# A diffusion step on one core: in the last feed-forward, the hi weights meet hi and lo of the operand in one product of 512 columns

## The chip, the cores and the metric

The kernel runs on one core of a Trainium2 chip. The metric is the device time of one execution in microseconds (us). Three executions of the kernel before took 2309.35, 2310.64 and 2311.0 us; the median is 2310.64 us.

## The reference

One inference step of a transformer trunk of two layers on two groups of 128 tokens each: context tokens and latent tokens, with the same weights. D_MODEL is 2048, D_FF is 5632. Every layer is a mixer (attention) followed by a gated feed-forward with a convolution over positions, each with its own shift, scale and gate from the conditioning:

```python
def conv_ffn(h, w_up, w_conv, b_conv, w_down):
    u = h @ w_up
    up = jnp.pad(u, ((0, 0), (1, 1), (0, 0)))
    u = up[:, :-2] * w_conv[0] + up[:, 1:-1] * w_conv[1] + up[:, 2:] * w_conv[2] + b_conv
    gate, val = u[..., :D_FF], u[..., D_FF:]
    return (jax.nn.silu(gate) * val) @ w_down
...
        x = x + gt1 * m
        h = rmsnorm(x, g_norm_ffn[l]) * (1 + sc2) + sh2
        x = x + gt2 * conv_ffn(h, w_ffn_up[l], w_ffn_conv[l], b_ffn_conv[l], w_ffn_down[l])
    return rmsnorm(x, g_final), ab_ctx, c_ctx
```

All inputs and outputs are float32. The change concerns the feed-forward of the second and last layer.

## The kernel before

**Operands in two parts.** The matmuls run on the type F32R, which keeps fewer bits than float32. So each operand is split into a hi part (the value rounded to F32R, an ACT copy, line 245) and a lo part (the remainder, a DVE subtraction, line 246). A product is the sum of three: hi weights on hi operand, hi weights on lo operand, lo weights on hi operand. Activations lie features on partitions, tokens along the free dimension: NT = 256 columns, 128 of each group. For each block k of 128 features, `hx[:, k, :NT]` is hi, `hx[:, k, NT:2 * NT]` is lo, and the two lie side by side in a row of ROW = 512 columns. The inner tiles `g` of the feed-forward have the same layout.

**One product.** `gemm` (from line 345) makes one block of 128 output features: it takes a bank of PSUM, `acc`, of which there are three in rotation, and issues for each of the 16 or 22 blocks of weights three matmuls of 256 columns into the first half of the bank. The second half of the bank stays unused. The matmul is issued at line 107, which is a helper, so all products have that line in the profile; they are told apart by the tile names: `hx` in the up-projection, `g` in the down-projection.

**Weights.** `Weights` loads them by DMA on SP's queue in tiles of 16 blocks (`raw`, three buffers), and splits half a tile (8 blocks, 1024 columns) at a time into `wh` and `wl`, which have four buffers each. A split of new weights waits until TensorE has finished with the oldest of the four.

**The feed-forward.** `ffn` (line 1452) runs `up(q)` and `down(gs, q)` for q = 0 and 1, each with half of the 5632 inner features. `up` makes 22 pairs of products (gate and value) of 16 blocks; `conv` takes each product through an ACT activation out of PSUM (line 1482) and two DVE operations that add the shifted neighbours (lines 1485 and 1488), then comes the gate's Silu (line 1504), a multiplication (line 1505), and a split into a tile `g`. `down` makes 16 products of 22 blocks; `residual` adds each one, times its gate, to `x` with two DVE operations that read PSUM (line 830), one for each group. In q = 1 the squares of `x` are also summed for the final normalisation. The last four products of `down` in q = 1 are "quiet": their weights are split in finer pieces.

**Other products.** The first four products of `up(0)` come from the normalisation before (`ready`, up to 258 columns wide). Five more products of `up(0)` begin with a matmul that is 32, 16, 8, 4 or 2 columns wider (`WIDER`). In the attention of the first layer there are products of 384 columns, on the tile `kv_in`.

**Beside it.** In the feed-forward DVE also sums vectors of the modulation from rows of `w_ada` (line 460, 2.3 us each). In the last layer these are needed by the residuals of `down(0)`.

**Order.** The order of the instructions on each engine is set by the framework's planner from its own estimate of their times; only instructions passed to `keep_order` keep the program's order.

Of the kernel before, what the change touches and what calls it, by code (L numbers as in the profile page):

```python
# [14 lines left out]
ALU = mybir.AluOpType  # L15
# [3 lines left out]
P = 128  # L19
# [3 lines left out]
NT = 2 * T  # L23
ROW = 2 * NT
SHIFT = 320
NL = 2
# [65 lines left out]
def step_kernel(ctx: ExitStack, tc: tile.TileContext, A: dict):  # L92
    nc = tc.nc
    dve, act, pool, sp = nc.vector, nc.scalar, nc.gpsimd, nc.sync
    kept = []

    def keep_order(i):
        if not any(i is j for j in kept):
            kept[:] = [i]
            tc.keep_in_program_order(i)  # L100
# [16 lines left out]
    pe = TensorE()  # L117
# [3 lines left out]
    tmp = ctx.enter_context(tc.tile_pool(name="tmp", bufs=2))  # L121
    small = ctx.enter_context(tc.tile_pool(name="small", bufs=4))
    pacc = ctx.enter_context(tc.tile_pool(name="pacc", bufs=3, space=PSUM))
# [5 lines left out]
    def banks(name):  # L129
        return tc.tile_pool(name=name, bufs=1, space=PSUM)  # L130
# [3 lines left out]
    def nm(s):  # L134
        uid[0] += 1
        return f"{s}_{uid[0]}"

    def T_(pl, shape, tag, dt=F32, bufs=None):
        kw = {} if bufs is None else {"bufs": bufs}
        return pl.tile(shape, dt, tag=tag, name=nm(tag), **kw)  # L140
# [11 lines left out]
    def C(name):  # L152
        a, w = _AT[name]
        return cst[:, a:a + w]
# [89 lines left out]
    def split(out_hi, out_lo, src, pin=lambda i: i):  # L244
        pin(act.copy(out_hi, src))  # L245
        pin(dve.tensor_tensor(out=out_lo, in0=src, in1=out_hi.bitcast(F32), op=ALU.subtract))  # L246
# [98 lines left out]
    def gemm(blocks, xh, xl, n=NT, first=0, between=None, more=None):  # L345

        fixed = lambda i: keep_order(i) if between is not None else i
        ps = T_(pacc, [P, 512], "acc")  # L350
        last = len(blocks) - 1
        for i in range(last + 1):
            k = (i + first) % (last + 1)
            wh, wl = blocks[k]
            x0 = more(k) if more and i == 0 else xh(k)
            fixed(pe.matmul(ps[:, :x0.shape[-1]], wh, x0, start=(i == 0), stop=False))
            if callable(between):
                if i == (last + 1) // 2:
                    between()
            elif between and i in between:  # L360
                between[i]()
            fixed(pe.matmul(ps[:, :n], wh, xl(k), start=False, stop=False))
            fixed(pe.matmul(ps[:, :n], wl, xh(k), start=False, stop=(i == last)))
        return ps[:, :n]

# [78 lines left out]
    def load_row():  # L446
        feat["row"] = T_(feat["home"], [P, 2, D], "condb")
        sp.dma_start(out=feat["row"], in_=A["condb"])
        for r in range(2):
            keep_order(act.activation(feat["row"][:, r], feat["row"][:, r], AF.Silu))  # L450
# [30 lines left out]
    class Deep:  # L481
# [44 lines left out]
        def pump(self):  # L526
            self.due += self.rate
            while self.due >= 1.0:
                self.due -= 1.0
                if self.steps:  # L530
                    self.step()
# [82 lines left out]
    def ensure(l, j, qs=range(4)):  # L614
        for u in [(l, j, q) for q in qs]:
            while u in ROWS and u not in done and ada["i"] <= ROWS.index(u):
                row_step()
            while u in FEATS and u not in done:
                feature_step()
            while u in DEEP[l] and u not in done:  # L620
                deep.step()
            while u not in done:
                later.pop(0)()
# [92 lines left out]
    def operand(pl, tag):  # L716
        return home(pl, tag)[:, :KD * ROW].rearrange("p (k n) -> p k n", k=KD)

    def raw_tile(pl, tag):
        return home(pl, tag)[:, :KD * 2 * UW].rearrange("p (k n) -> p k n", k=KD)  # L720
# [731 lines left out]
    def ffn(hx, W, ready, turn, l, st):  # L1452
        xh, xl = (lambda k: hx[:, k, :NT]), (lambda k: hx[:, k, NT:2 * NT])
        wider = list(WIDER)
        long = len(ready) > 3

        def product():
            if ready:
                return ready.pop(0)
            if in_order:  # L1460
                return gemm(W.chunk(), xh, xl, between=in_order.pop(0))
            if wider:
                n = NT + wider.pop(0)
                return gemm(W.chunk(), xh, xl, more=lambda k: hx[:, k, :n])
            return gemm(W.chunk(), xh, xl)

        WD = Weights(A["w_down"][l], KQ, TB)
        cw = ada["cw"]
        with tc.tile_pool(name=f"ffn{l}", bufs=1) as fp, banks(f"pffn{l}") as pf:
            feat["home"], feat["pool"] = fp, pf  # L1470
            feat["due"] = 0.0
            in_order = [{}, {}] + turn + [{}]
            T_(fp, [P, SHIFT // 4], "pad")

            def conv(m):
                early = bool(ready)
                pin = keep_order if early else lambda i: i
                if len(ready) > 4 - 2 * long:
                    W.ahead(pin)
                ps = product()  # L1480
                y = T_(fp, [P, NT], "cv", bufs=3)
                pin(act.activation(y, ps, AF.Identity, scale=cw[:, 1, m:m + 1], bias=cw[:, 3, m:m + 1]))  # L1482
                y3 = y.rearrange("p (g t) -> p g t", g=2)
                p3 = ps.rearrange("p (g t) -> p g t", g=2)
                pin(dve.scalar_tensor_tensor(out=y3[:, :, 1:], in0=p3[:, :, :T - 1],  # L1485
                                             scalar=cw[:, 0, m:m + 1], in1=y3[:, :, 1:],
                                             op0=ALU.mult, op1=ALU.add))
                pin(dve.scalar_tensor_tensor(out=y3[:, :, :T - 1], in0=p3[:, :, 1:],  # L1488
                                             scalar=cw[:, 2, m:m + 1], in1=y3[:, :, :T - 1],
                                             op0=ALU.mult, op1=ALU.add))  # L1490
                if early and ready and not long:
                    W.ahead(pin)
                return y

            def up(q):
                gs = []
                for i in range(q * KQ, (q + 1) * KQ):
                    rate = 0 if i < LATE else FRATE["up"]
                    fine[0] = False
                    gate = conv(i)  # L1500
                    pump(0, rate)
                    val = conv(NFF + i)
                    pump(0, rate)
                    act.activation(gate, gate, AF.Silu)
                    dve.tensor_tensor(out=val, in0=gate, in1=val, op=ALU.mult)
                    g = T_(fp, [P, ROW], "g", F32R, bufs=KQ)
                    split(g[:, :NT], g[:, NT:2 * NT], val)
                    gs.append(g)
                    if i == LATE - 1:
                        load_row()  # L1510
                return gs

            def down(gs, q):
                u, rows = None, None
                if q == NQ - 1 and l < NL - 1:
                    u = raw_tile(keep, "hx")
                    rows = raw_rows(u, l + 1, 0)
                for c in range(KD):
                    quiet = q == NQ - 1 and c >= KD - QUIET[0]
                    fine[0] = quiet  # L1520
                    if q == 0:
                        ensure(l, 5, [c // 4])
                    ps = gemm(WD.chunk(), lambda k: gs[k][:, :NT], lambda k: gs[k][:, NT:2 * NT])
                    if l == NL - 1 and q == NQ - 1 and c == KD - 1:
                        last_residual(ps, l, 1, c, st)
                    else:
                        residual(ps, l, 1, c, st if q == NQ - 1 else None)
                    if rows:
                        rows(c)
                    if l == NL - 1 and q == NQ - 1 and c in EARLY:  # L1530
                        act.activation(x[:, c], x[:, c], AF.Identity, scale=C("gfin")[:, c:c + 1])
                    pump(0, 0 if quiet else FRATE["down"])
                return u

            for q in range(NQ):
                gs = up(q)
                u = down(gs, q)
            while feat["i"] < FLIMIT[stage[0]]:
                feature_step()
            return u  # L1540


    with banks("pab") as ppool["ada"]:
# [3 lines left out]
        ps = T_(pacc, [P, 512], "acc")  # L1547
# [5 lines left out]
        hx = operand(keep, "hx")  # L1553
        st = stat_init()
        with tc.tile_pool(name="beside", bufs=1) as beside:
            o = mixer_ab(hx, beside)
            with tc.tile_pool(name="raw", bufs=1) as rp:
# [3 lines left out]
                W = Weights(A["w_up"][0], KD, 1)  # L1561
# [5 lines left out]
    with tc.tile_pool(name="cc", bufs=1) as cp, banks("pc") as ppool["ada"]:  # L1567
# [3 lines left out]
        W = Weights(A["w_in_c"], KD, 1)  # L1571
# [5 lines left out]
        W = Weights(A["w_up"][1], KD, 1)  # L1577
# [149 lines left out]
```

## Time and profile before

| what | value |
|---|---|
| median of three executions | 2310.64 us |
| profiled execution, its own time | 2308.48 us |
| its span, first to last instruction | 2306.7 us |
| last feed-forward in the chain of waits | 1579.00 to 2294.34 us |
| transfers, mean over the span | 268 GB/s, queue of the loads 72.3% busy |
| granted clock of TensorE, mean | 0.996 |

In a page of the profile PE is TensorE's matmuls, PEld its weight loads, DVE VectorE, ACT ScalarE, POOL GpSimd, SP SyncE. A group of instructions is given by source line, engine, operation, output and input tile, shape and count; then its busy time, the mean of one in ns, and the idle time of the engine just before it with what ended it. A row of the timeline is start, duration, instruction, and how many were merged into the row. A matmul's duration includes the way through the array; the pace is read from the distance of two starts. A row of the stretches of time gives for each engine the busy time and the number of instructions, then the granted clock, the share of busy transfer engines and GB/s.

### The profile page before, as it was taken

How to read it: one execution, taken by the hardware profiler on the slowest of the kernel's cores; microseconds unless marked ns; L12 is line 12 of the kernel's file. 1: busy time of each engine (PE TensorE's matmuls, PEld its weight loads, DVE VectorE, ACT ScalarE, POOL GpSimd, SP SyncE). 2: the span in 40 equal slices, each digit the busy share in tenths (PEclk: the TensorE clock that was granted, in tenths of full speed). 3: DMA queues.
4: the chain of work that ended last, by engine and by line, in shares of the span. 5: the costliest groups of instructions: out<-in, count | busy, mean ns of one | idle time of the engine just before them, and what ended most of it. 6: DMA issues, size and time to landing. Idle time of an engine off the chain costs nothing.

```text
span 2306.7 us, 47528 instructions
## 1 busy us (share of the span) xinstructions
PE 2278.7 (99%) x19504; PEld 2186.1 (95%) x19504; DVE 1887.0 (82%) x2967; ACT 1202.5 (52%) x1973; POOL 188.5 (8%) x238
## 2 busy tenths in 40 slices
PE   8999999999999999999999999999999999999998
PEld 6788878999999999999999999999999999999998
DVE  4667979889999999999988988898899965666654
ACT  4346555665553355555575455457555434555543
POOL 0011211400000000001130000023000000000011
PEclk9999999999999999999999999999999999999999
DMA  9988888777777777777787888776677755555553
GB/s 379 378 334 304 313 326 332 280 275 264 263 256 288 290 276 258 270 264 256 286 310 283 309 316 312 271 268 227 247 256 260 264 200 190 200 190 194 198 188 127
DMA packets 100122, 617.15 MB, mean 268 GB/s; under 512 B 10752, under 2 KB 18880, under 8 KB 33344
## 3 DMA queue, kind: packets, MB, share of 16 engines
q1 hardware_dynamic: 99904, 614.11, 72.3%
q8 instruction: 153, 2.51, 0.4%
q14 instruction: 65, 0.53, 0.1%
HBM read 609.32 MB, written 4.75 MB: 266 GB/s over the span
## 4 chain that ended last, share of the span: by engine, by line
PE 84%; DMA 0%; DVE 0%; ACT 0%; POOL 0%; issue 0%; DVEq 0%; ACTq 0%
PE acc L107 81%; PE ada L107 1%; PE att L107 1%; PE att L110 0%; DMA araw<-w_ada 0%; DVE x L1589 0%; PE ada L110 0%; PE misc L107 0%; DVE wl L246 0%; ACT wh L245 0%; POOL rr L219 0%; DVE hx L246 0%; ACT hx L245 0%; ACT p L862 0%; PE misc L110 0%
## 5 line engine op out<-in xcount | busy, mean ns | idle before, releaser
L107 PE MATMUL acc<-hx,wh 128*128 128x256 f32 (+1 forms) x7264 | 1256.2, 278 | 3.6 <-ACT wh L245 1.7
L245 ACT CAST wh<-raw 128x1024 fp32r<-128x1024 f32 (+2 forms) x828 | 796.1, 972 | 871.3 <-PE acc L107 744.1
L246 DVE TENSOR_TENSOR wl<-raw,wh 128x1024 fp32r<-128x1024 f32 (+2 forms) x828 | 923.2, 1130 | 252.8 <-ACT wh L245 247.8
L107 PEld LDWEIGHTS acc<-hx,wh 128*128 128x128 f32 x7264 | 1100.4, 188 | 23.6 <-issue 8.3
L107 PE MATMUL acc<-hx,wl 128*128 128x256 f32 (+1 forms) x3632 | 1007.1, 277 | 4.7 <-DVE wl L246 4.7
L107 PEld LDWEIGHTS acc<-hx,wl 128*128 128x128 f32 x3632 | 684.5, 188 | 8.5 <-DVE wl L246 6.0
L107 PE MATMUL acc<-g,wh 128*128 128x256 f32 x2816 | 478.8, 276 | 0.0
L107 PEld LDWEIGHTS acc<-g,wh 128*128 128x128 f32 x2816 | 423.8, 188 | 0.0
L107 PE MATMUL acc<-g,wl 128*128 128x256 f32 x1408 | 388.0, 276 | 0.0
L460 DVE CUSTOM_DVE_ANT_0 junk<-araw,condb 128x2048 f32<-128x2048 f32 x128 | 294.1, 2297 | 0.0
L107 PE MATMUL acc<-hxc,wh 128*128 128x256 f32 (+1 forms) x1568 | 282.9, 282 | 0.0
L107 PEld LDWEIGHTS acc<-g,wl 128*128 128x128 f32 x1408 | 264.2, 188 | 0.0
L107 PEld LDWEIGHTS acc<-hxc,wh 128*128 128x128 f32 x1568 | 241.5, 189 | 4.5 <-issue 4.2
L107 PE MATMUL acc<-hxc,wl 128*128 128x256 f32 (+1 forms) x784 | 218.5, 279 | 0.0
L208 POOL TENSOR_TENSOR sqacc<-sqacc,sq 128x256 f32<-128x256 f32 x62 | 72.8, 1174 | 1493.8 <-ACT sq L204 1493.7
L107 PEld LDWEIGHTS acc<-hxc,wl 128*128 128x128 f32 x784 | 147.5, 188 | 0.4
L1482 ACT ACTIVATE cv<-acc,convw 128x256 f32<-128x256 f32 x169 | 94.4, 559 | 0.0
L512 DVE CUSTOM_DVE_ANT_0 hx<-block,condb 128x1024 fp32r<-128x1024 f32 x65 | 79.2, 1218 | 9.0 <-DMA block<-w_ada 6.4
L1488 DVE SCALAR_TENSOR_TENSOR cv<-acc,convw,cv 128x254 f32<-128x254 f32 x169 | 80.8, 478 | 3.2
L830 DVE SCALAR_TENSOR_TENSOR x<-acc,mod,x 128x128 f32<-128x128 f32 x190 | 57.1, 341 | 30.4 <-PE acc L107 30.4
L1485 DVE SCALAR_TENSOR_TENSOR cv<-acc,convw,cv 128x254 f32<-128x254 f32 x169 | 80.1, 474 | 0.0
L107 PE MATMUL ada<-araw,condw 128*32 128x512 f32 (+1 forms) x608 | 73.8, 578 | 1.3 <-DMA araw<-w_ada 1.3
(262 smaller groups left out, 1542.4 us busy)
## 6 DMA issues: line engine op xcount, KB each, us to landing
raw<-w_up SPq DMA_DIRECT2D x176, 1024.0 KB, 4.8
araw<-w_ada SPq DMA_DIRECT2D x136, 1024.0 KB, 5.9
raw<-w_down SPq DMA_DIRECT2D x88, 1024.0 KB, 4.8
raw<-w_in_c SPq DMA_DIRECT2D x48, 1024.0 KB, 6.7
block<-w_ada SPq DMA_DIRECT2D x41, 512.0 KB, 6.4
raw<-w_in_ab SPq DMA_DIRECT2D x18, 1024.0 KB, 9.2
raw<-w_out_ab SPq DMA_DIRECT2D x16, 1024.0 KB, 7.1
raw<-w_out_c SPq DMA_DIRECT2D x16, 1024.0 KB, 6.4
```

Of the source, the lines that this page charges most:

```text
L107: return self.placed(nc.tensor.matmul(*a, **kw))
L208: eng.tensor_tensor(out=st["acc"], in0=st["acc"], in1=sq, op=ALU.add)
L245: pin(act.copy(out_hi, src))
L246: pin(dve.tensor_tensor(out=out_lo, in0=src, in1=out_hi.bitcast(F32), op=ALU.subtract))
L460: keep_order(dve.tensor_tensor_reduce(out=T_(feat["pool"], [P, D], "junk"), in1=feat["row"][:, c], in0=feat["raw"].rearrange("p g n -> p ( ...
L512: keep_order(dve.tensor_tensor_reduce(out=self.junk, in0=self.raw, in1=self.row[:, c].rearrange("p (g n) -> p g n", g=2), scale=1.0, scala ...
L830: dve.scalar_tensor_tensor(out=x[:, c, s], in0=ps[:, s], scalar=mod[:, l, 3 * which + 2, c, g:g + 1], in1=x[:, c, s], op0=ALU.mult, op1=AL ...
L1482: pin(act.activation(y, ps, AF.Identity, scale=cw[:, 1, m:m + 1], bias=cw[:, 3, m:m + 1]))
L1485: pin(dve.scalar_tensor_tensor(out=y3[:, :, 1:], in0=p3[:, :, :T - 1], scalar=cw[:, 0, m:m + 1], in1=y3[:, :, 1:], op0=ALU.mult, op1=ALU.add))
L1488: pin(dve.scalar_tensor_tensor(out=y3[:, :, :T - 1], in0=p3[:, :, 1:], scalar=cw[:, 2, m:m + 1], in1=y3[:, :, :T - 1], op0=ALU.mult, op1=A ...
```

## The change

The new function `gemm_pairs` issues two matmuls for each block of weights in place of three. The hi weights meet all 512 columns of the operand's row, hi and lo, and fill both halves of the bank; the lo weights meet hi and add to the first half. For the last block the order of the two is turned round. Then ACT copies the second half to a tile of SBUF (`nt`, four buffers, which exists before) and DVE adds the first half to it. The caller gets this tile where it got PSUM before.

It is used in the last layer alone, from its first `down` on: 16 products of `down(0)`, 44 of `up(1)` and 12 of `down(1)`. The four quiet products at the end remain as they are.

```diff
+    def gemm_pairs(blocks, both):
+
+        ps = T_(pacc, [P, 512], "acc")
+        last = len(blocks) - 1
+        for k in range(last + 1):
+            wh, wl = blocks[k]
+            two = [(ps, wh, both(k)), (ps[:, :NT], wl, both(k)[:, :NT])]
+            for i, (out, w, xs) in enumerate(two if k < last else two[::-1]):
+                pe.matmul(out, w, xs, start=(k == 0 and i == 0), stop=(k == last and i == 1))
+        t = T_(tmp, [P, NT], "nt", bufs=4)
+        act.copy(t, ps[:, NT:])
+        dve.tensor_tensor(out=t, in0=ps[:, :NT], in1=t, op=ALU.add)
+        return t
...
+        pairs = [False]
 
         def product():
             if ready:
...
+            if pairs[0]:
+                return gemm_pairs(W.chunk(), lambda k: hx[:, k, :ROW])
             return gemm(W.chunk(), xh, xl)
...
-                    ps = gemm(WD.chunk(), lambda k: gs[k][:, :NT], lambda k: gs[k][:, NT:2 * NT])
+                    if pairs[0] and not quiet:
+                        ps = gemm_pairs(WD.chunk(), lambda k: gs[k][:, :ROW])
+                    else:
+                        ps = gemm(WD.chunk(), lambda k: gs[k][:, :NT], lambda k: gs[k][:, NT:2 * NT])
...
             for q in range(NQ):
                 gs = up(q)
+                pairs[0] = l == NL - 1
                 u = down(gs, q)
```

## The prediction

> **What bounds the kernel now.** I read the page first: shares of the engines, then the chain of work that ended last.
>
> ```profile
> PE 2278.7 (99%) x19504; PEld 2186.1 (95%) x19504; DVE 1887.0 (82%) x2967; ACT 1202.5 (52%) x1973; POOL 188.5 (8%) x238
> ...
> PE acc L107 81%; PE ada L107 1%; PE att L107 1%; PE att L110 0%; DMA araw<-w_ada 0%; DVE x L1589 0%; PE ada L110 0%; PE misc L107 0%; DVE wl L246 0%; ACT wh L245 0%; POOL rr L219 0%; DVE hx L246 0%; ACT hx L245 0%; ACT p L862 0%; PE misc L110 0%
> ```
>
> TensorE is busy 99% of the span, and one line of matmuls is 81% of the chain. Next, the chain in order of time over the last stage:
>
> ```profile
> 1579.00 715.33 PE acc L107 x6296
> ```
>
> From 1579.00 us to 2294.34 us, which is the whole last feed-forward, the chain is matmuls and nothing else: no engine and no transfer makes TensorE wait. So what the change is worth is what it does to the pace of these matmuls, unless it makes another engine late. The stage splits into its parts so (TensorE, weight load, DVE, ACT, POOL busy, clock, DMA):
>
> ```profile
> 1579.00:1817.90 238.90, 238.90 (x2095) 238.90 (x2094) 220.02 (x308) 142.99 (x221) 19.09 (x24) 1.00 0.70 252
> 1817.90:1847.90 30.00, 30.00 (x267) 30.00 (x266) 27.05 (x33) 11.80 (x12) 0.00 (x0) 1.00 0.68 250
> 1847.90:1937.60 89.70, 89.70 (x794) 89.70 (x793) 51.38 (x63) 34.81 (x33) 0.00 (x0) 1.00 0.56 199
> 1937.60:2176.90 239.30, 239.30 (x2114) 239.30 (x2113) 161.52 (x217) 127.30 (x175) 0.00 (x0) 1.00 0.56 194
> 2176.90:2266.60 89.70, 89.70 (x794) 89.70 (x793) 48.82 (x64) 41.51 (x53) 13.74 (x11) 1.00 0.56 196
> ```
>
> The rows are: first half of the up-projection with the end of the normalisation, the first four products of the first down-projection (DVE still has modulation vectors to sum), its other twelve, the second half of the up-projection, and the twelve products of the second down-projection that the change takes. The granted clock is 1.00 in all of them.
>
> **The pace.** The timeline of TensorE gives the start of each triple (hi weights on hi, hi weights on lo, lo weights on hi):
>
> ```profile
> 1899.76 0.39 PE L107 MATMUL acc<-g,wh 128*128 128x256 f32 x2
> ...
> 1905.88 0.39 PE L107 MATMUL acc<-g,wh 128*128 128x256 f32 x2
> ```
>
> Eighteen triples lie between these two rows: 6.12 us / 18 = 340.0 ns, 113.3 ns for a matmul. What of that is columns streaming? Early on the clock was granted at half, and there the same matmul went so:
>
> ```profile
> 26.00:30.00 4.00, 4.00 (x20) 4.00 (x20) 1.38 (x3) 2.06 (x5) 0.00 (x0) 0.50 1.01 422
> ...
> 25.31 0.63 PE L107 MATMUL acc<-hx,wh 128*128 128x256 f32 x2
> ...
> 29.79 0.63 PE L107 MATMUL acc<-hx,wh 128*128 128x256 f32 x2
> ```
>
> Seven triples in 4.48 us are 213.3 ns a matmul at clock 0.50. I take this as pure streaming, so 106.7 ns for 256 columns at full clock, 0.4167 ns a column. Over that the present pace pays 6.7 ns a matmul, 20 ns a triple. This surcharge is all that there is to win: the columns that stream stay 768 for each block of weights.
>
> **What the change removes and adds.** It takes 72 products: 16 of the first down-projection (22 blocks each), 44 of the second up half (16 blocks), 12 of the second down-projection (22 blocks); the last four stay as they are. That is 352 + 704 + 264 = 1320 triples that become pairs, one matmul of 512 columns and one of 256. 1320 matmuls and as many weight loads go. With S5 and S2 for the surcharges of the wide and the narrow one, a pair takes 320.0 + S5 + S2, and the difference for the run is 1320 x (S5 + S2 - 20.0) ns.
>
> No matmul of the 512-column kind with these operands is in the trace, so I bound S5 and S2. The nearest rows in width, on the same sort of operand, are the 384-column products, in two places:
>
> ```profile
> 219.97 0.51 PE L107 MATMUL acc<-kv_in,wh 128*128 128x384 f32 x2
> ...
> 221.01 0.51 PE L107 MATMUL acc<-kv_in,wh 128*128 128x384 f32 x2
> ...
> 246.01 0.51 PE L107 MATMUL acc<-kv_in,wh 128*128 128x384 f32 x2
> ...
> 247.60 0.51 PE L107 MATMUL acc<-kv_in,wh 128*128 128x384 f32 x2
> ```
>
> Two triples in 1.04 us: 173.3 ns a matmul; three in 1.59 us: 176.7 ns. Streaming is 160.0, so the surcharge is 13.3 to 16.7 ns, twice that of the 256-column ones, though the weights have far more time to load. The narrow shapes, too, mostly pay more than 6.7:
>
> ```profile
> 1579.44 0.41 PE L107 MATMUL acc<-hxc,wh 128*128 128x258 f32 x2
> ...
> 1584.83 0.40 PE L107 MATMUL acc<-hxc,wh 128*128 128x258 f32 x2
> ...
> 1597.07 0.41 PE L107 MATMUL acc<-hx,wh 128*128 128x256 f32 x2
> ...
> 1606.61 0.40 PE L107 MATMUL acc<-hx,wh 128*128 128x256 f32 x2
> ```
>
> 258 columns: 15 triples in 5.39 us, 119.8 ns, surcharge 12.3. And 256 columns right behind them: 27 triples in 9.54 us, 117.8 ns, surcharge 11.1. So one and the same shape has two steady paces, 113.3 and 117.8. What happens when a row of the quick pace is broken by one wider matmul shows here:
>
> ```profile
> 482.45 0.41 PE L107 MATMUL acc<-hx,wh 128*128 128x288 f32 x2
> 482.69 0.28 PE L107 MATMUL acc<-hx,wl 128*128 128x256 f32 x1
> 482.81 0.41 PE L107 MATMUL acc<-hx,wh 128*128 128x256 f32 x2
> 483.06 0.28 PE L107 MATMUL acc<-hx,wl 128*128 128x256 f32 x1
> 483.17 0.39 PE L107 MATMUL acc<-hx,wh 128*128 128x256 f32 x2
> ```
>
> From 482.45 to 483.17 are six matmuls with 1568 columns: 653.3 ns of streaming in 720 ns, 11.1 ns of surcharge each; only then the quick pace is back. I read this as: the low surcharge belongs to unbroken rows of 256 columns, and any other rhythm pays 11 to 17 ns a matmul. A pair changes width at every matmul.
>
> So S5 is taken from the 384-column rows, 13.3 (to 16.7), and S2 between the slow 256 and the 258 rows, 11.8 (11.1 to 12.3). The pair is 226.7 + 118.5 = 345.2 ns, 5.2 more than the triple: **1320 x 5.2 = +6.9 us**. The ends of this reading: 24.4 - 20.0 = 4.4 ns, +5.8 us, and 29.0 - 20.0 = 9.0 ns, +11.9 us. The far bounds for any reading: downward, a wide matmul that pays hardly anything. Plain f32 operands of 512 columns stood at the start of the run:
>
> ```profile
> 8.05 1.02 PE L107 MATMUL acc<-am 128*128 128x512 f32 x2
> ...
> 8.05 4.03 PE L107 MATMUL acc<-am 128*128 128x512 f32 x9
> ```
>
> Two of them take 1.02 us from the first start to the last end and nine take 4.03, so seven starts fill 3.01 us: 430.0 ns each, which I read as twice the stream of 512 columns (426.7) and 3.3 ns. With S5 = 3 and S2 = 6.7 the pair is 329.7, -13.6 us. Upward, the step from 256 to 384 columns goes on (60.0 ns for 128 columns from 113.3 to 173.3, so 233.3 for 512) beside the 258 rows' 12.3: 352.3 ns, +16.2 us.
>
> The last four products keep 264 triple matmuls; if they fall to the slow pace, 264 x 4.4 = +1.2 us; I take 0, as the break above healed within six matmuls.
>
> **What the way out adds.** Each product now passes through an ACT copy and a DVE addition, before the convolution or the residual reads it. Nearest rows, from the second up half and the first four down products:
>
> ```profile
> L246 DVE TENSOR_TENSOR wl<-raw,wh 128x1024 fp32r<-128x1024 f32 x88 | 107.9, 1226 | 75.6 <-ACT wh L245 73.0
> L245 ACT CAST wh<-raw 128x1024 fp32r<-128x1024 f32 x88 | 92.9, 1055 | 112.5 <-PE acc L107 86.3 <-issue 26.2
> L1482 ACT ACTIVATE cv<-acc,convw 128x256 f32<-128x256 f32 x44 | 24.5, 558 | 0.0
> L1488 DVE SCALAR_TENSOR_TENSOR cv<-acc,convw,cv 128x254 f32<-128x254 f32 x43 | 20.7, 482 | 1.5
> ...
> L460 DVE CUSTOM_DVE_ANT_0 junk<-araw,condb 128x2048 f32<-128x2048 f32 x6 | 13.7, 2291 | 0.0
> ```
>
> I price the copy at 0.56 us and the addition at 0.48 us. In the second up half that is 44 x 0.56 = 24.6 us on ACT's 127.3 and 44 x 0.48 = 21.1 us on DVE's 161.5, in 239.3 us: both keep room. The cover is the lead of the weights: each half tile holds 8 blocks (2.72 us of matmuls), there are four, and ACT waits for TensorE to free one (the 86.3 us above), so a cast and a subtraction (1.06 + 1.23 us) have three half tiles, 8.2 us, to finish. An ACT copy that waits for the product's last matmul holds back the next cast behind it, and the DVE addition the next subtraction, by a microsecond at most, inside these 8.2. The accumulator's bank is held about 1 us longer than ACT's copy needs to begin, with two other banks, over 10 us of matmuls, ahead of the next use. So these cost nothing; with the cover gone they would cost 72 x 1.04 = 75 us. No DMA is moved, and SP's and POOL's queues are not passed by anything.
>
> **Against the forecast.** The trace's 256-column row is 113.3 ns. The Trainium skill, page "TensorE: Matmul & The Clock Gate", section "Back-to-back issue gap", has the gap of matmuls at full clock as their columns at 2.4 GHz and 2.5 ns; an estimate from that page is 215.8 ns for 512 columns, with the measured 113.3 a pair of 329.1 and -14.4 us. It speaks for the change; the 384-column rows, 10.8 to 14.2 ns above that rule, do not bear it out.
>
> **The rivals.**
> 1. *Every matmul pays the same 6.7 ns and a third of them is saved* (the other side). For it: in the broken row above the 288-column matmul and its successor (482.45 to 482.69, 544 columns, 226.7 ns of streaming) pay some 13 ns together, the low surcharge still, and 512 is two times 256, so that the quick rhythm might hold. Against: the 384 rows, in which no repetition brings it about. The pair is 333.3, -6.7 ns x 1320 = -8.8 us: 2301.8 us. The rule of the Trainium skill's page above would be its far end. It decides from S5 + S2 below 20.
> 2. *The wide one pays as 384 columns do, the narrow one keeps its quick pace*: 226.7 + 113.3 = 340.0 ns, no change, 2310.6 us. The same time results if the wide product is split into two of 256 columns on its way to the chip, so that nothing is saved.
> 3. *DVE becomes the bound where it still sums modulation vectors*: 27.05 us of 30.00 in the first four down products, and 4 x 0.48 = 1.9 us come on top, 28.97 in all, without the waits between them. If all 1.9 us were exposed on top of the forecast: 2319.4 us. It decides when the additions push subtractions past the 8.2 us lead.
>
> **How the numbers follow.** The profiled execution has a span of 2306.7 us and a time of 2308.5 us; the median shown is 2310.64 us, 2.2 us more. The pace is read from the former, and as a difference it goes onto the median: 2310.6 + 6.9 = **2317.5 us**, own range 2316.4 to 2322.5. A measurement can tell some 0.2% (4.6 us) from no change, 3.5 ns in the pair. Chances: forecast 0.45, rival 1 0.31, rival 2 0.21, rival 3 0.03. Rival 2 is all within 0.2%; the forecast and rival 3 are slower by more, except the forecast's lower tail, 0.03; of rival 1 some 0.01 falls within: faster 0.30, same 0.25, slower 0.45. The range takes in rival 1 down to 2298.5 us, short of the downward bound of 2297.0 (some 0.08 left out below), and reaches up to 2325, short of the upward bound of 2326.8 (0.05 left out).
>
> **What would show it.** Right: 1320 matmuls fewer on TensorE's count, 128x512 forms under the wide line, and pair after pair some 345 ns apart in the timeline with no idle time of TensorE. 333 ns is rival 1, 340 rival 2; a TensorE that waits for lo weights around 1820 to 1850 us is rival 3. The step most likely to be wrong is S5, which stands on one other width in another stage.

## The result and the profile after

The changed kernel takes 2326.79 us (median of 4 runs, 2325.93 to 2327.56) against 2309.99 us for the kernel before beside it (2308.38 to 2311.0). The ratio is 1.0073, 95% interval 1.0056 to 1.0091: slower by 16.8 us. The forecast was 2317.5 us with a range up to 2325.0; the direction was right, the loss was more than twice what was forecast.

The page of the changed kernel, shares of the engines, and the long piece of its chain of waits in order of time (start, us, what):

```profile
PE 2295.2 (99%) x18184; PEld 2140.4 (92%) x18184; DVE 1914.4 (82%) x3039; ACT 1224.8 (53%) x2045; POOL 189.1 (8%) x238
```

```profile
1581.04 732.42 PE acc L107 x4976
```

TensorE has 1320 matmuls and 1320 weight loads less (18184 for 19504), as counted, and the last feed-forward is still one unbroken row of matmuls: nothing has come between. That row lasts 732.42 us in place of the 715.33 of before. It is 17.1 us longer with 21% fewer instructions, so the loss is in the pace. The timeline of TensorE, changed kernel, with the starts of the wide matmuls of one product of the first down-projection:

```profile
1895.46 0.39 PE L107 MATMUL acc<-g,wh 128*128 128x512 f32 x1
1895.69 0.28 PE L107 MATMUL acc<-g,wl 128*128 128x256 f32 x1
1895.81 0.40 PE L107 MATMUL acc<-g,wh 128*128 128x512 f32 x1
...
1899.70 0.40 PE L107 MATMUL acc<-g,wh 128*128 128x512 f32 x1
```

Twelve pairs lie between the first and the last row: 4.24 us, 353.3 ns a pair, 13.3 more than the 340.0 of the triple. By the starts in ns the wide matmul has 235.0 of it and the narrow one 118.3. 1320 x 13.3 ns = 17.6 us. The row's 17.1 us are 12.9 ns a pair; a little is saved at the turn from one product to the next, where two wide ones meet and the first of them takes 233.3. The two groups of wide matmuls, by form:

```profile
L107 PE MATMUL acc<-hx,wh 128*128 128x512 f32 x704 | 245.4, 397 | 0.0
L107 PE MATMUL acc<-g,wh 128*128 128x512 f32 x616 | 215.7, 397 | 0.0
```

Their idle time before is 0.0, as it was for the groups of 256 columns. What the way out costs its engines:

```profile
L376 ACT COPY nt<-acc 128x256 f32<-128x256 f32 x72 | 26.9, 373 | 94.4 <-PE acc L107 94.4
...
L377 DVE TENSOR_TENSOR nt<-acc,nt 128x256 f32<-128x256 f32 x44 | 18.7, 424 | 37.5 <-ACT nt L376 37.5
```

(The second row is of the second up half alone.) 0.37 and 0.42 us for each product, a little less than priced, and neither is waited for by TensorE.

### The profile page after: what moved, and what is told of

Read it like the earlier page. It is cut to its first block, busy times and chain, and to the rows that moved or that the text cites. A ratio compares the mean times of both kernels' runs of the same rounds, so it can differ in the third digit from the quotient of the medians.

```text
span 2325.6 us, 44926 instructions
## 1 busy us (share of the span) xinstructions
PE 2295.2 (99%) x18184; PEld 2140.4 (92%) x18184; DVE 1914.4 (82%) x3039; ACT 1224.8 (53%) x2045; POOL 189.1 (8%) x238
## 4 chain that ended last, share of the span: by engine, by line
PE 84%; DMA 0%; DVE 0%; ACT 0%; POOL 0%; issue 0%; DVEq 0%; ACTq 0%
PE acc L107 81%; PE ada L107 1%; PE att L107 1%; PE att L110 0%; DMA araw<-w_ada 0%; DVE x L1610 0%; PE ada L110 0%; DVE wl L246 0%; PE misc L107 0%; ACT wh L245 0%; POOL rr L219 0%; DVE hx L246 0%; ACT hx L245 0%; ACT p L876 0%; PE misc L110 0%
## 5 line engine op out<-in xcount | busy, mean ns | idle before, releaser
L107 PE MATMUL acc<-hx,wh 128*128 128x256 f32 (+2 forms) x6560 | 1259.8, 291 | 4.6 <-ACT wh L245 1.7
L107 PEld LDWEIGHTS acc<-hx,wh 128*128 128x128 f32 x6560 | 1015.4, 188 | 53.2 <-issue 10.1
L107 PE MATMUL acc<-g,wh 128*128 128x256 f32 (+1 forms) x2200 | 484.9, 310 | 0.0
L107 PEld LDWEIGHTS acc<-g,wh 128*128 128x128 f32 x2200 | 352.3, 188 | 25.8
L376 ACT COPY nt<-acc 128x256 f32<-128x256 f32 x72 | 26.9, 373 | 94.4 <-PE acc L107 94.4
L1499 ACT ACTIVATE cv<-acc,convw 128x256 f32<-128x256 f32 x125 | 69.7, 558 | 0.0
L377 DVE TENSOR_TENSOR nt<-acc,nt 128x256 f32<-128x256 f32 x72 | 30.4, 422 | 45.4 <-ACT nt L376 45.4
L1505 DVE SCALAR_TENSOR_TENSOR cv<-acc,convw,cv 128x254 f32<-128x254 f32 x125 | 59.6, 477 | 1.6
```

The lines of the kernel that those rows point to most:

```text
L107: return self.placed(nc.tensor.matmul(*a, **kw))
L376: act.copy(t, ps[:, NT:])
L377: dve.tensor_tensor(out=t, in0=ps[:, :NT], in1=t, op=ALU.add)
```

## The experiments

All are the changed kernel with the edit shown, unless it is said otherwise. The kernel before took 2308.9 to 2309.8 us beside them (medians). A time without an interval is that of a single run, and the paces are read from one profile each.

**Three matmuls again, the way out kept.**

```diff
-            two = [(ps, wh, both(k)), (ps[:, :NT], wl, both(k)[:, :NT])]
+            two = [(ps[:, :NT], wh, both(k)[:, :NT]), (ps[:, NT:], wh, both(k)[:, NT:]),
+                   (ps[:, :NT], wl, both(k)[:, :NT])]
```

> The changed kernel, but the hi weights meet hi and lo of the operand in two matmuls of 256 columns, one into each half of the bank; the way out (ACT copy, DVE addition) stays. Theory A (the width of the wide matmul costs, the way out nothing): the triple is 340 ns again, and the time is that of before within 0.2%, about 2310 us. Theory B (writing and reading the second half of the bank, or the ACT copy and the DVE addition, costs): the pace stays well above 340 ns or TensorE shows idle time, and most of the 16.8 us remain, about 2320 us or more.

2308.59 us, ratio to before 0.9997 (0.9987 to 1.0006). The chain of waits:

```profile
1579.02 715.33 PE acc L107 x6296
```

To the hundredth of a microsecond the 715.33 us of before. The second half of the bank, the copy and the addition cost nothing; all of the loss is in the 512-column matmul and what it does to the narrow one. Theory B has fallen.

**Other widths.** One run holds three of them.

```diff
+            two = [(ps[:, :w5], wh, both(k)[:, :w5]), (ps[:, :NT], wl, both(k)[:, :NT])]
...
+                return gemm_pairs(W.chunk(), lambda k: hx[:, k, :ROW], 384)
+                        ps = gemm_pairs(WD.chunk(), lambda k: gs[k][:, :ROW], 320 if q == 0 else 448)
```

> The changed kernel with a narrower wide matmul: 320 columns in the first down-projection, 384 in the second up half, 448 in the second down-projection (the columns behind these of lo are left out of the product). The pair of the changed kernel is 353.3 ns. Theory A (operand columns stream at 60 ns for each 128, 0.469 ns a column, and the pair has 6.7 ns less than that): 263.3, 293.3 and 323.3 ns a pair. Theory B (columns stream at 0.417 ns, and a pair pays a fixed surcharge of 33.3 ns for its change of width): 273.3, 300.0 and 326.7 ns.

The timeline, first and last wide matmul of a stretch for each width:

```profile
1879.81 0.31 PE L107 MATMUL acc<-g,wh 128*128 128x320 f32 x1
...
1883.49 0.31 PE L107 MATMUL acc<-g,wh 128*128 128x320 f32 x1
...
2000.63 0.33 PE L107 MATMUL acc<-hx,wh 128*128 128x384 f32 x1
...
2003.78 0.33 PE L107 MATMUL acc<-hx,wh 128*128 128x384 f32 x1
...
2189.89 0.36 PE L107 MATMUL acc<-g,wh 128*128 128x448 f32 x1
...
2191.81 0.36 PE L107 MATMUL acc<-g,wh 128*128 128x448 f32 x1
```

14 pairs in 3.68 us, 11 in 3.15 and 6 in 1.92: 262.9, 286.4 and 320.0 ns, where streaming alone would be 240.0, 266.7 and 293.3. The surcharge of a pair is 23, 20 and 27 ns, and 33 with 512. A fixed one of 33 ns (theory B) has fallen. Theory A meets the first within a nanosecond and is 7 and 3 ns too high for the others: the surcharge grows with the width, though not evenly.

**Only wide matmuls.**

```diff
-            two = [(ps, wh, both(k)), (ps[:, :NT], wl, both(k)[:, :NT])]
+            two = [(ps, wh, both(k)), (ps, wl, both(k))]
```

> The changed kernel with both matmuls of a pair 512 columns wide (the lo weights meet hi and lo too, which adds the product of lo and lo). Theory A (0.469 ns a column): each is 233 to 235 ns, a pair 466.7 to 470, and the time is some 167 us above before, about 2477 us. Theory B (it is the change of width that costs, one width alone keeps a surcharge of 6.7 ns): 220 ns each, 440 a pair, some 132 us above before, about 2442 us.

2477.62 us, and in the timeline:

```profile
1999.80 0.39 PE L107 MATMUL acc<-hx,wh 128*128 128x512 f32 x1
...
2002.60 0.39 PE L107 MATMUL acc<-hx,wh 128*128 128x512 f32 x1
```

Twelve matmuls in 2.80 us, 233.3 ns each, with no change of width anywhere. (Matmuls with hi and with lo weights take 231 and 236 in turn.) 113.3, 173.3 (the attention's products of before in one place; 176.7 in the other) and 233.3 ns for 256, 384 and 512 columns are steps of some 60 ns for 128 columns, where the stream alone takes 53.3. The surcharge goes with the columns, some 6.7 ns for each 128 from 256 on, and is not a fixed one of the matmul.

**The order turned round.** First all wide matmuls of a product, then the narrow ones.

```diff
+        order = [(0, k) for k in range(last)] + [(1, k) for k in range(last + 1)] + [(0, last)]
+        for i, (low, k) in enumerate(order):
+            n = NT if low else 2 * NT
+            pe.matmul(ps[:, :n], blocks[k][low], both(k)[:, :n], start=(i == 0), stop=(i == 2 * last + 1))
```

> The changed kernel with the order turned round: first all wide matmuls of a product, then all narrow ones, so that the width changes twice a product and not 32 or 44 times. Theory A (the width itself costs 20.0 ns on 512 columns, and the change of width some 6.7 ns a pair): 233.3 and 113.3 to 118 ns, a pair 346.7 to 351, the time about 9 to 14 us above before, 2319 to 2324 us, and less than the changed kernel's 16.8. Theory B (all of the 13.3 ns a pair is the change of width): 340 ns or less a pair, no more than before, about 2310 us. If TensorE waits for weights in it, the pace alone is read.

2320.49 us, ratio 1.0048 (1.0033 to 1.0062): 10.7 us above before, six less than the changed kernel. TensorE does not wait in it; the chain, and one product of 16 blocks in the timeline, read:

```profile
1580.43 725.48 PE acc L107 x4976
...
2050.71 2.96 PE L107 MATMUL acc<-hx,wh 128*128 128x512 f32 x12
2053.51 1.98 PE L107 MATMUL acc<-hx,wl 128*128 128x256 f32 x16
2055.32 2.96 PE L107 MATMUL acc<-hx,wh 128*128 128x512 f32 x12
```

Twelve wide ones from 2050.71 to 2053.51 are 233.3 ns each, sixteen narrow ones to 2055.32 are 113.1. So of the changed kernel's 13.3 ns a pair the columns have 6.7, and the order, in which the widths take turns, the other 6.7: 1.7 on the wide one, 5.0 on the narrow one, which regains its quick pace in a row of its own. The narrow one's 118.3 is close to the slow pace of 117.8 that unbroken rows of 256 columns have too; that a change of width is the only thing that takes the quick pace away is not shown, and the run with bf16 down-projections below speaks against it. The last four products, which no edit touches, ran at 113.3 ns a matmul in the changed kernel and at 117.8 here: 264 x 4.5 = 1.2 of the 10.7 us.

**Operands of two bytes.** Weights and operand of the two down-projections in bf16.

```diff
+                        cols, kind = (2048, BF16) if self.bf else (1024, F32R)
+                        wh_ = T_(wpool, [P, cols], "wh", kind, bufs=4)
+                        wl_ = T_(wpool, [P, cols], "wl", kind, bufs=4)
...
+        WD = Weights(A["w_down"][l], KQ, TB, bf=(l == NL - 1))
+                    g = T_(fp, *(([P, 2 * ROW], "g", BF16) if l == NL - 1 else ([P, ROW], "g", F32R)), bufs=KQ)
```

> The changed kernel with weights and operand of both down-projections of the last layer in bf16 in place of F32R (two bytes a value; hi and lo together then keep fewer bits). The same 512 and 256 columns go into the same f32 banks. Theory A1 (reading four bytes a column is what slows the stream): 512 columns take about 216 ns and 256 about 109 to 113, a pair 325 to 330. Theory A2 (the slowness is on the way into the bank, or belongs to the width alone): the pair stays at about 353 ns. Either way the second up half, which stays F32R, keeps 353 ns.

```profile
1899.92 0.38 PE L108 MATMUL acc<-g,wh 128*128 128x512 bf16 x1
...
1902.85 0.38 PE L108 MATMUL acc<-g,wh 128*128 128x512 bf16 x1
```

Nine pairs in 2.93 us, 325.6 ns; by the starts in ns 216.0 and 109.0. The columns, the banks and the f32 results are the same, so neither the width nor the way into the bank is slow by itself: it goes with the type of what is read, columns or weights. The second up half kept its 353 ns, and the run's 2309.36 us are the sum: 704 x 13.3 = +9.4 us there, 616 x (325 - 340) = -9.2 us in the down-projections. The Trainium skill's page "TensorE: Matmul & The Clock Gate", section "Back-to-back issue gap", gives the gap of isolated matmuls at full clock as their columns at 2.4 GHz and 2.5 ns; an estimate from it is 215.8 and 109.2 ns. The trace agrees for bf16, and for F32R the 233.3 and 113.3 are 17.5 and 4.1 ns above.

**The same few columns again and again.** The wide matmul reads the first n columns of the row 512 / n times.

```diff
-            two = [(ps, wh, both(k)), (ps[:, :NT], wl, both(k)[:, :NT])]
+            two = [(ps, wh, both(k)[:, None, :n].to_broadcast([P, 2 * NT // n, n])), (ps[:, :NT], wl, both(k)[:, :NT])]
```

> The changed kernel, but the wide matmul reads the first 8 columns of the operand's row 64 times in place of 512 different columns (the product is left without most of its operand). As many columns stream and as many results are written. Theory A (four-byte values go to the array at a limited rate, wherever they lie): 234 to 235 ns, as before. Theory D (walking through the row's addresses, 2 KB of them beside the weights' addresses, makes the collisions): the wide one falls to 214 to 220 ns.

> As the run with 8 columns read 64 times (216 ns), but with more different columns: the first 32 of the row 16 times in the first down-projection, the first 128 four times in the second up half, the first 256 twice in the second down-projection (most of the operand is left out). Theory C (collisions with the weights' reads as the operand walks through its addresses): the wide matmul rises from 216 ns with 32 to some 230 ns or more with 128 and 256. Theory D2 (only the length of the row read, 2 KB, is what costs): all three stay near 216 ns.

> Between 8 columns read 64 times (216 ns) and 32 read 16 times (237 ns): the first 4 columns of the row in the first down-projection, 16 in the second up half, 64 in the second down-projection. Theory A (each new stretch of 32 bytes of four-byte columns that is fetched costs a part of a clock): 4 stays at 216 ns, 16 and 64 are at 230 ns or above. Theory C (collisions with the weights by place): 16 columns, 64 bytes, lie apart from most of the weights' reads and stay near 216 to 220 ns, 64 are between.

| n, four-byte columns | 4 | 8 | 16 | 32 | 64 | 128 | 256 | 512 (all) |
|---|---|---|---|---|---|---|---|---|
| wide matmul, ns (mean to the next start, over the stage) | 216.3 | 216.0 | 243.4 | 236.8 | 234.8 | 234.6 | 234.8 | 234.5 |

The row of 8 and that of 16, each in the second up half:

```profile
1999.95 0.38 PE L107 MATMUL acc<-hx,wh 128*128 128x512 f32 x1
...
2003.28 0.38 PE L107 MATMUL acc<-hx,wh 128*128 128x512 f32 x1
```

```profile
2049.83 0.41 PE L107 MATMUL acc<-hx,wh 128*128 128x512 f32 x1
...
2050.93 0.41 PE L107 MATMUL acc<-hx,wh 128*128 128x512 f32 x1
```

Ten pairs in 3.33 us against three in 1.10: 333 and 367 ns. Four-byte columns stream at the pace of bf16 ones (216.0) as long as the matmul stays within 32 bytes, and from 64 bytes on they do not. So the four bytes themselves are no hindrance on the way through the array; the loss comes with the fetching, once it goes beyond those 32 bytes. Theory D was right that 8 columns are quick, but it is not the length of 2 KB that counts, since 64 bytes cost as much. The narrow matmul stays at 117 to 123 ns beside all of them.

**Is it a collision with the reading of the next weights?** Two ways: fewer columns of weights (the other outputs are left out), and operands that lie elsewhere.

```diff
+            two = [(ps[:64], wh[:, :64], both(k)), (ps[:64, :NT], wl[:, :64], both(k)[:, :NT])]
```

> Weights of 64 columns, so that a weight load reads half as much (half of each product's outputs is left out). The down-projections run pairs of 512 and 256 columns, the second up half runs triples of 256 with such weights. Theory A (reading the four-byte operand is slow by itself): the pair stays at 353 ns with 234 to 235 for the wide one, and the triple is 340 ns or above. Theory C (what slows the operand's stream is the reading of the next weights beside it, which are four bytes a value too): with half the weights to read the surcharge of 33 ns a pair falls by about half, to 336 ns or less, and the triple falls below 340 towards 325 ns.

> The changed kernel with fewer columns of weights in a pair: 32 in the first down-projection, 64 in the second up half, 96 in the second down-projection (the other outputs are left out). Columns that stream and operand reads stay. Theory C (each read of weights takes time from the operand's reads): with 128 columns the wide one is 235 ns and with 64 it was 228, so about 224 with 32 and 231 with 96, in proportion. Theory A (four-byte operand lines are slow by themselves, and the 228 belong to another rhythm): 228 or more with 32 columns, without proportion.

The timelines, first for 64 columns in pairs, then for 64 in triples of 256, both of the first of these runs:

```profile
1900.59 0.39 PE L107 MATMUL acc<-g,wh 128*64 128x512 f32 x1
...
1903.36 0.39 PE L107 MATMUL acc<-g,wh 128*64 128x512 f32 x1
```

```profile
2050.18 0.40 PE L107 MATMUL acc<-hx,wh 128*64 128x256 f32 x2
...
2053.04 0.40 PE L107 MATMUL acc<-hx,wh 128*64 128x256 f32 x2
```

Eight pairs in 2.77 us: 346 ns, with 228 for the wide one. Eight triples in 2.86 us: 357.5 ns, slower than the 340.0 with all weights. But that is 119.2 ns a matmul, near the slow pace of 117.8 that whole weights have too, so this rise is not shown to come from the weights. The second run gives for the wide matmul 229.6 ns (32 columns, values from 224 to 239), 228.0 (64) and 233.3 (96). So with a quarter of the weights 16 of the 21.7 ns remain, and there is no proportion: theory C is not borne out as the main cause, though fewer weights do change the rhythm by some 6 ns. The Trainium skill, page "TensorE: Matmul & The Clock Gate", section "Step-by-step: what each phase is for", says that loading the next weights takes no read bandwidth from the running matmul; the 235 to 228 ns are a small sign to the contrary, the missing proportion speaks for it.

```diff
+                    off = 0 if l < NL - 1 else 4 * (i % KQ) if q == 0 else 8 * (i % KQ) % 128
+                    g = T_(fp, [P, ROW + 128 * l], "g", F32R, bufs=KQ)[:, off:off + ROW]
```

> The changed kernel, but in the last layer each tile of the down-projection's operand begins at a place of its own: block k lies k x 16 bytes further on than before in the first down-projection (0 to 336 bytes), k x 32 bytes, modulo 512, in the second. Nothing else changes, and the weights stay. Theory C (the operand's reads collide with those of the next weights, by their places in the memory): the time of a wide matmul goes up and down with k, somewhere down to 216 to 225 ns, somewhere above 235. Theory A (four-byte columns are slow wherever they lie): 233 to 235 ns for each k, within 2 ns.

```profile
1580.18 732.49 PE acc L107 x4976
```

By the starts in ns the wide matmul goes from 225 to 241 ns with the block's place, nearly the same from product to product after the first few, with a mean of 232.6 in the first down-projection and 232.8 in the second. The row of matmuls lasts as long as in the changed kernel (732.42), and the time is 2326.68 us. So place shifts it by up to 8 ns either way. That is the up and down that theory C expected, with its low end at 225, and more than theory A's 2 ns; but none of the 27 places comes near 216, and the mean hardly moves. Collisions by place are a part of it, and the runs do not show that they are the whole.

**Corrections alone in bf16.** The kernel before, with three matmuls of 256 columns in the last two down-projections, two of them on bf16 copies.

```diff
+            pe.matmul(ps[:, :NT], wh, hi(k), start=(k == 0), stop=False)
+            pe.matmul(ps[:, :NT], whb, lo(k), start=False, stop=False)
+            pe.matmul(ps[:, :NT], wl, hib(k), start=False, stop=(k == last))
```

> The kernel before, with three matmuls of 256 columns a block, but in the last layer's two down-projections the two corrections (hi weights on lo operand, lo weights on hi operand) run on bf16 copies; only hi on hi stays F32R. Theory A (four-byte values are what holds TensorE above the stream of columns): the bf16 ones take 109 ns each, the triple 327 to 332 ns in place of 340, 704 triples, 6 to 9 us below before, about 2302 to 2304 us. Rival: each change between the types costs what the bf16 saves, or ACT's 88 additional casts make TensorE wait: 2310 us or more.

2319.9 us, ratio 1.0040 (1.0026 to 1.0054), slower. The chain and the timeline of a few blocks:

```profile
1581.28 724.72 PE acc L108 x6296
...
1900.16 0.39 PE L108 MATMUL acc<-gb,wl 128*128 128x256 bf16 x2
1900.31 0.36 PE L108 MATMUL acc<-g,wh 128*128 128x256 f32 x1
1900.51 0.39 PE L108 MATMUL acc<-gb,wl 128*128 128x256 bf16 x2
...
1901.92 0.39 PE L108 MATMUL acc<-gb,wl 128*128 128x256 bf16 x2
```

Five blocks from 1900.16 to 1901.92 are 352 ns each. The matmul between the types begins late: from the F32R one to the next bf16 one it is 0.20 us. The rival was right that a change of type costs more than bf16 saves; its other half, that ACT's casts make TensorE wait, did not occur, for the row of matmuls is unbroken.

**Down-projections wholly in bf16, the up half as before.**

```diff
-            if pairs[0]:
-                return gemm_pairs(W.chunk(), lambda k: hx[:, k, :ROW])
```

(beside the bf16 edit shown above)

> The second up half as in the kernel before (triples of 256 columns in F32R), the last layer's two down-projections in bf16 (hi and lo of weights and operand keep fewer bits), in pairs of 512 and 256 columns but for the last four products, which are triples. From the run with bf16 pairs: 325 ns a pair and 109 ns a matmul of 256. 616 x (325 - 340) = -9.2 us and 264 x 4.3 = -1.1 us: about 2299 us, 0.45% below before. If the bf16 kernel's gain is eaten up elsewhere: 2310 us.

2308.7 us, ratio 0.9998 (0.9989 to 1.0008): the gain is gone. Stretches of the second up half, in this run and in the next one:

```profile
1980.00:2150.00 170.00, 170.00 (x1446) 170.00 (x1445) 111.58 (x151) 86.69 (x121) 0.00 (x0) 1.00 0.53 186
```

```profile
1980.00:2150.00 170.00, 170.00 (x1502) 170.00 (x1501) 115.85 (x156) 90.23 (x125) 0.00 (x0) 1.00 0.54 193
```

In 170 us there are 1446 matmuls of 256 columns here (117.6 ns each) where the quick pace gives 1500. They never left the slow pace, though nothing in this half changes width: 704 x 3 x 4.4 ns = 9.3 us, which eats the bf16 gain of 10.3.

**The same, with five products that begin a little wider.**

```diff
             for q in range(NQ):
+                if q and l == NL - 1:
+                    wider.extend(WIDER)
                 gs = up(q)
```

> The run with bf16 down-projections gained some 10 us there, but the triples of 256 columns in the second up half went at 117.8 ns in place of 113.3 and gave 9 us back. Here the first five products of that half begin with a matmul that is 32, 16, 8, 4 or 2 columns wider, as the first half's products do. Theory E (256-column triples have two steady paces, and a single wider matmul can bring them from the slow one to the quick one): 113.3 ns after a few products, about 2300 us, 0.4% below before. Theory F (the slow pace comes from what lies around, bf16 or the operand's place): 117.8 ns throughout, about 2309 us.

2298.43 us, ratio 0.9954 (0.9940 to 0.9968), the fastest of the runs that leave nothing of the product out, at fewer bits in the last layer's down-projections. The second fence above is its row: 1502 matmuls, 113.2 ns. The timeline shows where the pace changes:

```profile
1939.58 0.40 PE L108 MATMUL acc<-hx,wh 128*128 128x256 f32 x2
...
1940.29 0.40 PE L108 MATMUL acc<-hx,wh 128*128 128x256 f32 x2
1940.64 0.40 PE L108 MATMUL acc<-hx,wh 128*128 128x264 f32 x2
...
1941.35 0.39 PE L108 MATMUL acc<-hx,wh 128*128 128x256 f32 x2
1941.69 0.39 PE L108 MATMUL acc<-hx,wh 128*128 128x256 f32 x2
```

Two triples before the third of the five wider matmuls take 0.71 us, the third triple of its own product 0.34. The first two wider ones, of 288 and 272 columns, had not done it. So at one matmul of 264 columns some 2000 others went over from one pace to the other; theory E holds, theory F has fallen. Why this one, and what set the slow pace, is open.

## Why the prediction was wrong in size

**What bounds it** was right: matmuls before, matmuls after, nothing beside them on the path. **The count** of 1320 was right.

**The way out at nothing** was right: the run with three matmuls and the way out kept has before's chain of 715.33 us. Rival 3, DVE as the bound, did not occur.

**The last four products at nothing** came true (113.3 ns a matmul), but not by a rule that the runs bear out: with the order turned round the same products stayed at 117.8.

**S2**, the narrow matmul, was forecast at 11.8 ns over its stream and measured 11.7 (118.3). The reading behind it, that a rhythm broken by another width loses the quick pace, agrees with the run with the order turned round, in which it is back. That only unbroken rows have the quick pace is right as far as the runs go; that unbroken rows have it always is not, as the 117.6 ns of the run with bf16 down-projections show.

**S5** is the step that failed: "So S5 is taken from the 384-column rows, 13.3 (to 16.7)". It measured 21.7. The forecast took the surcharge as one of the matmul, of the same size at any width, from "any other rhythm pays 11 to 17 ns a matmul". The runs show one of the columns: some 60 ns for 128 of them, so that 512 cost 233.3 with no change of width at all, and 235.0 with it. With S5 = 21.7 the forecast's own sum is 21.7 + 11.8 - 20.0 = 13.5 ns a pair, 1320 x 13.5 = 17.8 us, against 16.8 measured. The prediction's own rows allowed this reading. Its slow ones, 117.8 ns for 256 columns and 176.7 for 384, are both 0.460 ns a column; 512 at that are 235.6 and a pair 353.4, where 235.0 and 353.3 came. (This is a working from two rows and no shown rule: pairs of 320, 384 and 448 columns would take 265.0, 294.4 and 323.8 by it, and took 262.9, 286.4 and 320.0.) The step from 113.3 to 173.3 leads the same way, and the prediction had it as its upward bound ("the step from 256 to 384 columns goes on"), 352.3 ns where 353.3 came; but it left only 0.05 of the chances above its range, which ended 1.8 us below the result.

**Rivals 1 and 2** needed a wide matmul of 220.0 and of 226.7 ns, both beside a narrow one of 113.3. With all weights and all columns in F32R the wide one took 235.0 and came to some 225 only for single places of the operand; 113.3 came in rows of narrow matmuls, and not with the widths in turn.

What stays open is why the fetching of four-byte columns loses some 6.7 ns for each 128 columns once a matmul reads more than 32 bytes of a row, and how much of it is the weights' reading: 64 columns of weights took 7 ns off, 32 took no more, and place moved it by 8 ns either way. No run has weights of one type and columns of another, and none has matmuls without a weight load of their own. It is open, too, what puts rows of 256 columns on the one or the other of their two paces.

## What to carry to other kernels

Fewer and wider matmuls are worth only what their surcharge gives back: price a new width from at least two others of the same operand type and look whether the surcharge goes with the matmul or with the columns. Here four-byte columns cost some 60 ns for each further 128 and narrow ones already ran at 113.3 ns for 256, so saving a third of the weight loads saved nothing. A pace in the trace can have two steady values for one shape; check which one is on after every edit ahead of it.

## What the runs showed of the hardware that was not expected

- F32R columns at granted clock 1.00: 113.3, 173.3 and 233.3 ns for 256, 384 and 512 (117.8, 176.7 and 235.0 in other places); bf16: 109.0 and 216.0 for 256 and 512; F32R with 8 columns read 64 times: 216.0.
- Triples of 256 columns with half the weights were not quicker: 357.5 ns against 340.0 with all.
- A change between bf16 and F32R in a block costs more than 20 ns: 352 ns for a triple that would be 331 by its single matmuls (113.3 + 2 x 109.0).
- At one matmul of 264 columns the 256-column stream went from 117.6 to 113.2 ns.
